# The second layer's projected inputs: inside attention, or at the head of the first feed-forward layer

## The chip, the cores and the metric

The kernel runs on one core of a Trainium2 chip. A core has five engines, each with its own queue of instructions that it works through in order: TensorE (PE, matrix products; its weight loads, PEld, overlap them), VectorE (DVE, element-wise work), ScalarE (ACT, activation functions and copies), GpSimd (POOL) and SyncE (SP, which issues nearly all transfers here). An instruction waits at the head of its queue for the results it needs and holds up all that stands behind it. Products are summed in PSUM, eight banks of 128 × 512 numbers; PE cannot write a bank again before another engine has read it.

The metric is the device time of one launch in microseconds (us). Before the change: 1715.05 us, the median of 3 runs (1713.93 to 1715.07).

## What is computed

A small encoder of two layers, 768 tokens in all (sequences of 512 and 256, kept side by side), model width 1024. Layer 0 mixes tokens by windowed attention, layer 1 by a gated convolution; each is followed by a feed-forward layer (1024 to 4096, squared rectifier, back to 1024) and by a gated input of its own:

```python
for i in range(DEPTH):
    h = rms_norm(x, norm_mix[i])
    x = x + (window_attention(h, ...) if i % 2 == 0 else short_conv(h, ...))
    h = rms_norm(x, norm_mlp[i])
    x = x + jnp.square(jax.nn.relu(h @ mlp_w_up[i])) @ mlp_w_down[i]
    gate = jax.nn.sigmoid(rms_norm(x, norm_ple[i]) @ ple_w_gate[i])
    x = x + (p[i] @ ple_w_proj[i]) * gate
return rms_norm(x, final_norm)
```

`p[i] @ ple_w_proj[i]`, the projected inputs, is a product of 768 × 256 by 256 × 1024. It depends on nothing else in the program, so it can be computed anywhere before the last step of its layer. The change concerns `p[1] @ ple_w_proj[1]`, which is needed near the end of the kernel.

## The kernel before

**Precision.** Every operand of a large product is split into a high part (a copy by ScalarE in a reduced format, L83 or L409) and a low part (the rest, a subtraction on VectorE, L84 or L420). A product is three matmuls: high by high, high by low, low by high.

**Layout.** Activations lie transposed: eight blocks of 128 channels × 768 tokens. In attention a product covers the tokens as 512 + 256 (`group`, L138), everywhere after it as two halves of 384 in two banks (`both`, `group2`, L129).

**Projected inputs.** `step` (L486) computes one block of 128 output channels: 12 weight loads, each streaming all tokens. The result is copied out of PSUM by ScalarE (or VectorE, for half of the first layer's) and stored to DRAM (`pj`), from where `gated` (L1109) fetches it much later. The first layer's eight steps are done at the very start while inputs load. The second layer's stand in attention: the inputs are split after the last block of head group 0 (`inputs1`), and the eight steps come after the last block of head group 1 (`projected(0)`, `projected(1)`).

**Attention** works through four groups of heads with six blocks of 128 queries each (`attend`, L639). In a block, PE makes scores (L667, L668); VectorE adds the bias and finds the maximum (L669); ScalarE exponentiates (L689); VectorE and ScalarE scale (L697, L695); PE transposes (L702); ScalarE and VectorE split (L710, L711); PE multiplies by the values (L712, L713); ScalarE and VectorE move the sum to `heads` (L715, L720). Other work is listed in `beside` to be issued after certain blocks: queries, keys, projections, the first part of the output. In this part a scheduler orders the instructions of every engine by its own estimates, the listed place being only a preference. At the end a loop of eight output products (24 or 12 weight-and-half pairs, 144 matmuls in all) finishes the residual stream block by block, in the order of `PAIRED`; `norm.block` then squares, scales and splits each block for the feed-forward layer, and `behind(i)` hangs further work after the i-th block.

**Feed-forward layer** (`mlp`, L853). The order of ACT, PE and DVE is written by hand here (`manual_schedule`). The hidden width is worked through in 16 chunks of 256; after each two come two `down` products. A chunk is either plain (`up_plain`, L897: 96 matmuls of 384 tokens) or a product by Strassen's scheme with seven part products instead of eight (`up`, L956: 84 matmuls). The second kind needs sums of blocks of the weights (`sums32`, `sums14`: VectorE) and of the activations (`norm.combine`, L301: two scaled copies and two high parts on ScalarE, four additions and two low parts on VectorE, for each of four pairs of blocks). `PLAIN` says how many of the first chunks of each layer are plain: three in layer 0, two in layer 1. `weave` interleaves several chains of steps. Work of chunk u's output that needs not be done at once is kept in `pend` and issued during the next.

In layer 0 chunk 0 runs before the statistics of the norm (`rstd_steps`: ones-matmuls at L226, a table load, logarithm, exponential, one Newton step) are known; its own output is scaled after them, and the four `combine` steps are spread over chunks 0 and 1.

**Buffers that matter.** Raw weights: three buffers (`wraw`). Split weights: two (`whi`, `wlo`), and one more of each under the tags `z` and `v`. PSUM after attention: four banks of tag A (two pairs), two of C, two of B; a new pair of a tag waits until the old one has been read. The six buffers of `big` hold passing results.

Of the kernel before, what the change touches and what calls it, by code (L numbers as in the profile page):

```python
# [11 lines left out]
F32 = mybir.dt.float32  # L12
# [6 lines left out]
P = 128  # L19
D = 1024  # L20
KB = D // P
# [26 lines left out]
def trunk_kernel(ctx: ExitStack, tc: tile.TileContext, a: dict, out: bass.AP):  # L48
# [397 lines left out]
    def mixer_attention():  # L446
# [10 lines left out]
        def pair(j, name, dt=F32):  # L457
            return main.tile([P, 2, T], dt, tag=f"x{j}", name=name)
# [24 lines left out]
                yield ps[:, :n], o, o + n  # L483
                o += n

        def step(i, w, part, tag, vector):  # L486

            l, m = i // KB, i % KB
            if tag == "L":
                t = ap.tile([P, T], F32, tag="L", name="pjs", bufs=BL)  # L490
            else:
                t = big("pjs")
            for ps, o, e in products(terms_of(w, part, col=m % 4 * P)):
                if vector:
                    dve.tensor_copy(t[:, o:e], ps)
                else:
                    act.activation(t[:, o:e], ps, AF.Copy)
            nc.sync.dma_start(pj[l][m], t[:])

        with tc.manual_schedule(engines=order):  # L500
            w0 = wp.tile([P, CH], F32, name="wraw", bufs=3)
            p0 = []
            for k in range(2):
                c = slice(512 * k, 512 * k + 512)
                nc.sync.dma_start(w0[:, c], a["proj"][0, 0, :, c])
                t = big("p")
                nc.sync.dma_start(t[:], a["p"][0, :, k, :])
                p0.append(t)
            w1 = fetch(a["proj"][0, 1])
            nc.sync.dma_start(vec[:], a["vec"][:])  # L510
# [12 lines left out]
            lo = wp.tile([P, CH], F32R, name="wlo", bufs=2)  # L523
            part0 = [], []
            for k in range(2):
                c = slice(512 * k, 512 * k + 512)
                split(hi[:, c], lo[:, c], w0[:, c])
                ph, pl = slot(10 + k, "p0h"), slot(12 + k, "p0l")
                split(ph[:], pl[:], p0[k][:])
                part0[0].append(ph[:])  # L530
                part0[1].append(pl[:])
            w0 = blocks(hi[:], 2), blocks(lo[:], 2)
            w1 = weight(None, 2, raw=w1)
            for i in range(KB):
                step(i, (w0, w1)[i // 4], part0, "L", i % 2)
                norm.block(i, xin(i))
                if i == 3:
                    wk = weight(None, KB, raw=wk)
                    wq = [fetch(a["w_q"][0])]

            bp = psum.tile([P, 512], F32, tag="S", name="bp", bufs=2)
            pe.matmul(bp[:HEADS, :], lhsT=rb[:], rhs=oh[:], start=True, stop=True)
            brow = tmp.tile([HEADS, 512], F32, tag="t", name="brow")
            dve.tensor_tensor(brow[:], bp[:HEADS, :], mk[:], ALU.add)
            kps = list(products(terms_of(wk, xs)))
            wq[0] = weight(None, KB, raw=wq[0])
            ss = norm.sum_squares(psum)

        with s1:
# [206 lines left out]
            def keys1():  # L756
                keys(1, products(terms_of(weight(a["w_k"][1], KB), xs)))

            def projected(q):
                w = weight(a["proj"][1, q], 2)  # L760
                for i in range(4):
                    step(KB + 4 * q + i, w, part1, "t", False)

            part1 = [], []

            def inputs1():
                ps = [pair(2 + p, "p1", F32R) for p in range(2)]
                for k in range(2):
                    t = fetch(a["p"][1, :, k, :])
                    split(ps[0][:, k, :], ps[1][:, k, :], t[:, :T])  # L770
                    for p in range(2):
                        part1[p].append(ps[p][:, k, :])

            def begin_output():
                for g in range(2):
                    split_heads(g)


            beside = {
                (0, 5): (inputs1, keys1),  # L780
                (1, 5): (lambda: projected(0), lambda: projected(1)),
                (2, 5): (begin_output, first_output),
            }
            for g in range(KV - 1):
# [37 lines left out]
        return Weights7(a["up"][l, f], a["up"][l, f + 2], plain=u < PLAIN[l])  # L822


    PLAIN = 3, 2

    def weave(*chains):

# [21 lines left out]

    ET = mybir.EngineType

    def mlp(l, norm, nxt, w, places, early):  # L853


        xs = norm.xs
# [40 lines left out]
        def up_plain(u, w, make, then):  # L897

            nonlocal r

            ps = [both(f"p{i + 1}", {0: "AA", 1: "BC"}.get(u, "AA")[i]) for i in range(2)]
            y1 = y2 = None

            def rects(*which):
# [2 lines left out]


            order = [(0, (0, 6), (0, 1)), (1, (0, 6), (0, 1)), (0, (6, 8), (0, 1)), (1, (6, 8), (0, 1))]
            if u > 0:  # L910
                order = [(i, (0, 8), (o,)) for o in (1, 0) for i in range(2)]
            for n, (i, ks, sides) in enumerate(order):
                for k in range(*ks):
                    m, h = PAIRED[k] % (KB // 2), PAIRED[k] // (KB // 2)
                    c = slice(P * m, P * m + P)
                    hi, lo = w.w[f"w{i + 1}{h + 1}"]
                    for j, (wt, part) in enumerate(((hi, 0), (hi, 1), (lo, 0))):
                        for o in sides:
                            pe.matmul(
                                ps[i][o],  # L920
                                lhsT=wt[:, c],
                                rhs=xs[f"x{h + 1}{1 + o}"][m][part],
                                start=k == 0 and j == 0,
                                stop=k == KB - 1 and j == 2,
                            )
                if n == 0:
                    v = make()
                    split2 = [lambda: v.split("second")] if v.plain else []
                    todo1 = norm.combine(todo.pop(0)) if todo else []
                    rest, pend[:] = pend[:4], pend[4:]  # L930
                    weave(rest, todo1, split2)
                elif n == 1:
                    if r is None:
                        parts = norm.acc_parts()
                    sums = [] if v.plain else [v.sums32, v.sums14, lambda: v.split("direct")]
                    weave(norm.combine(todo.pop(0)) if todo else [], sums, pend)
                    pend.clear()
                elif n == 2:
                    v.split("direct" if v.plain else "s32")
                    if u > 0:  # L940
                        y1, y2 = big("y1"), big("y2")
                        rects((0, 1), (1, 1))
                else:
                    if r is None:
                        steps = norm.rstd_steps(psum, norm.sum_squares(psum, parts=parts, tag="C"))
                        weave(steps, norm.combine(todo.pop(0)) if len(todo) > 1 else [])
                        r = norm.r
                        y1, y2 = big("y1"), big("y2")
                        rects((0, 1), (1, 1))
                    rects((0, 0))  # L950
                    squared(y1)
                    rects((1, 0))
                    pend.extend(acts_of(u, y1, y2, y2))
# [122 lines left out]
                        add(m, ps[i])  # L1076
                        nxt.block(m, x(m))

        jobs = [(up_plain, 0), (up_plain, 1)]
        for g in range(NG - 1):  # L1080
            jobs += [(up if 2 * g + 2 >= PLAIN[l] else up_plain, 2 * g + 2), (down, g, 0), (down, g, 1), (up, 2 * g + 3)]
        with tc.manual_schedule(engines={ET.Activation, ET.PE, ET.DVE}):
            for i, (job, *args) in enumerate(jobs):

                def make():
# [145 lines left out]

    xs0 = [*range(32, 42), *range(8, 15), *range(16, 20), *range(7)]
    act0 = [7, *range(20, 24), 28, 29, *range(24, 28), 15, 30, 31]

    held = xs0[17:] + act0 + [xs0[16]]
# [2 lines left out]


    n1 = Norm7(2, "mlp0", xs0, act0[7:11], act0[11])
    w0, behind = first_chunk(0, n1, 0)
    w = [weight(a["w_o0"][2], 4), weight(a["w_o2"], 2)]
    for i, m in enumerate(PAIRED):
        if i == 4:
# [7 lines left out]
        n1.block(m, x(m))  # L1254
        behind(i)
    n2 = Norm(4, "ple0", xs0[:16], xs0[16])
    mlp(0, n1, n2, w0[0], act0, 0)
    n3 = Norm(1, "mix1", xs0[17:] + act0[:5], act0[5])
    ple(n2, n3, act0[6:9])

# [91 lines left out]
```

## Time and profile before

| | us |
|---|---|
| median of 3 runs | 1715.05 |
| the profiled execution | 1715.87 |
| its span, first to last instruction | 1714.1 |
| TensorE busy | 1672.0 (98%) |
| VectorE busy | 1339.6 (78%) |
| ScalarE busy | 855.7 (50%) |
| granted TensorE clock, mean | 0.992 |

The mean clock hides three short spells of half clock after the start: from 158.3 us for 3.4 us, from 349.4 for 10.2, and at the very end. Times in the profile count from the first instruction. In the lists below a row of a timeline holds start, duration, engine, line, operation, what it writes and reads (names without buffer numbers), shapes and a count of merged instructions; in brackets the idle time before it and what ended that. Matmuls are pipelined, so the duration of one is longer than the step from one to the next. A row of busy times holds the stretch, its length, and then, for PE, PEld, DVE, ACT and POOL in this order, busy time and number of instructions; then the granted clock, the share of the DMA engines and GB/s.

Attention's first block begins its product by the values at 82.60 us. The output loop starts at 285.22, the feed-forward layer at 310.37, and its first `down` product at 373.72.

### The profile page before, as it was taken

The numbers are of one execution on the slowest core, as the hardware profiler recorded it, in microseconds if no ns is written. First come the engines' busy times: TensorE is split into PE (matmuls) and PEld (weight loads), VectorE is DVE, ScalarE is ACT, GpSimd is POOL, SyncE is SP. The second block draws the span as 40 slices with busy tenths as digits, with TensorE's granted clock in tenths as the row PEclk, the third lists the DMA queues.
The fourth block names the chain that finished last, engine by engine and source line by source line (L and its number), as shares of the span: only waits on it lengthen the run. The fifth ranks groups of instructions, "written<-read, shape, count | busy, mean of one in ns | idle before, by whom it ended". The sixth has DMA issues, their size and how long they took to land. (4 is left out here: it accounts for less than half of the span.)

```text
span 1714.1 us, 24208 instructions
## 1 busy us (share of the span) xinstructions
PE 1672.0 (98%) x9554; PEld 1616.8 (94%) x9554; DVE 1339.6 (78%) x2198; ACT 855.7 (50%) x1363; POOL 2.0 (0%) x30
## 2 busy tenths in 40 slices
PE   8999999979999999999999999999999999999996
PEld 7887878979999999999999999999999999999986
DVE  7587788878999999977764444667989999999676
ACT  6467756645455455545541111445455555545454
POOL 0000000000000000000000000000000000000000
PEclk9999999989999999999999999999999999999998
DMA  8653331112221222122312121211221222222222
GB/s 263 189 146 110 114 109 62 45 50 74 65 84 62 75 74 74 62 84 93 108 62 62 62 62 62 76 60 49 74 73 64 74 75 74 65 71 86 74 89 96
DMA packets 47554, 143.80 MB, mean 84 GB/s; under 512 B 6048, under 2 KB 10656, under 8 KB 47440
## 3 DMA queue, kind: packets, MB, share of 16 engines
q1 hardware_dynamic: 44880, 139.10, 25.8%
q10 hardware_dynamic: 2560, 3.15, 0.7%
q8 instruction: 75, 1.23, 0.3%
q14 instruction: 39, 0.32, 0.1%
HBM read 122.31 MB, written 10.48 MB: 77 GB/s over the span
## 5 line engine op out<-in xcount | busy, mean ns | idle before, releaser
L83 ACT ACTIVATE whi<-wraw 128x1024 fp32r<-128x1024 f32 (+2 forms) x74 | 76.6, 1035 | 183.9 <-PE b L129 53.2
L409 ACT ACTIVATE whi<-sum 128x1024 fp32r<-128x1024 f32 x55 | 57.9, 1053 | 146.6 <-PE a L441 146.6
L866 ACT ACTIVATE y<-y 128x768 f32<-128x768 f32 x64 | 53.4, 838 | 140.5 <-DVE y L863 140.5
L84 DVE TENSOR_TENSOR wlo<-wraw,whi 128x1024 fp32r<-128x1024 f32 (+2 forms) x74 | 88.2, 1191 | 11.7 <-ACT whi L83 11.4
L441 PE MATMUL a<-act,whi 128*128 128x384 f32 x448 | 96.7, 337 | 0.0
L441 PE MATMUL a<-t,zhi 128*128 128x384 f32 x440 | 90.7, 337 | 1.8 <-ACT c L967 1.8
L441 PE MATMUL b<-t,zhi 128*128 128x384 f32 x440 | 90.5, 337 | 0.9 <-DVE y L863 0.9
L441 PE MATMUL a<-t,whi 128*128 128x384 f32 x440 | 90.5, 337 | 0.0
L1023 DVE TENSOR_TENSOR x<-x,a 128x384 f32<-128x384 f32 x112 | 60.8, 553 | 35.1 <-PE a L441 34.8
L441 PE MATMUL a<-xs,whi 128*128 128x384 f32 x432 | 84.5, 337 | 0.0
L138 PE MATMUL mm<-xs_mix,whi 128*128 128x512 f32 (+1 forms) x320 | 83.3, 342 | 0.0
L441 PEld LDWEIGHTS a<-t,zhi 128*128 128x128 f32 x440 | 77.9, 188 | 2.1 <-ACT c L967 2.1
L441 PEld LDWEIGHTS a<-act,whi 128*128 128x128 f32 x448 | 79.8, 188 | 0.0
L441 PEld LDWEIGHTS b<-t,zhi 128*128 128x128 f32 x440 | 77.7, 188 | 1.2 <-issue 1.2
L441 PEld LDWEIGHTS a<-t,whi 128*128 128x128 f32 x440 | 77.8, 188 | 0.0
L441 PEld LDWEIGHTS a<-xs,whi 128*128 128x128 f32 x432 | 76.3, 188 | 0.0
L420 DVE TENSOR_TENSOR wlo<-wraw,whi 128x1024 fp32r<-128x1024 f32 x60 | 73.0, 1217 | 1.9 <-ACT whi L409 1.9
L420 DVE TENSOR_TENSOR wlo<-sum,whi 128x1024 fp32r<-128x1024 f32 x55 | 67.2, 1222 | 9.2 <-ACT whi L409 9.2
L409 ACT ACTIVATE whi<-wraw 128x1024 fp32r<-128x1024 f32 x60 | 63.2, 1054 | 17.4 <-issue 10.3
L420 DVE TENSOR_TENSOR zlo<-sum,zhi 128x1024 fp32r<-128x1024 f32 x55 | 66.9, 1217 | 1.9 <-ACT zhi L409 1.9
L409 ACT ACTIVATE zhi<-sum 128x1024 fp32r<-128x1024 f32 x55 | 58.3, 1060 | 19.9 <-DVE sum L385 16.1
L330 ACT ACTIVATE t<-y 128x768 fp32r<-128x768 f32 x56 | 47.0, 841 | 40.6 <-DVE y L321 27.9
(279 smaller groups left out, 4647.9 us busy)
## 6 DMA issues: line engine op xcount, KB each, us to landing
wraw<-in_up SPq DMA_DIRECT2D x64, 512.0 KB, 3.5
wraw<-in_down SPq DMA_DIRECT2D x64, 512.0 KB, 3.5
wraw<-in_w_in SPq DMA_DIRECT2D x24, 512.0 KB, 3.4
wraw<-in_gate SPq DMA_DIRECT2D x16, 512.0 KB, 3.5
pj<-pjs SPq DMA_DIRECT2D x16, 384.0 KB, 2.9
wraw<-in_w_q SPq DMA_DIRECT2D x8, 512.0 KB, 4.9
wraw<-in_w_out SPq DMA_DIRECT2D x8, 512.0 KB, 3.4
x_in<-in_x SPq DMA_DIRECT2D x8, 384.0 KB, 7.2
```

Source lines behind the costliest of these rows:

```text
L83: first = act.activation(hi, src, AF.Copy)
L84: dve.tensor_tensor(lo, src, hi.bitcast(F32), ALU.subtract)
L138: pe.matmul(ps[:, o:e], lhsT=w, rhs=x[:, o:e], start=i == 0 and j == 0, stop=i == n - 1 and j == 2,)
L330: act.activation(t[0][:], (self.q1, self.q2)[i][:], AF.Copy)
L409: act.activation(hi[:], src, AF.Copy)
L420: dve.tensor_tensor(lo[:], src, hi[:].bitcast(F32), ALU.subtract)
L441: pe.matmul(ps, lhsT=a, rhs=b, start=start and i == 0, stop=i == len(terms) - 1, skip_group_check=True)
L866: act.activation(t[:], t[:], AF.Square)
L1023: dve.tensor_tensor(t[:, o : o + H], t[:, o : o + H], f, op)
```

## The change

The eight steps of the second layer's projected inputs leave attention and are issued between attention's output loop and the first chunk of layer 0's feed-forward part. Their inputs are loaded and split after the first two blocks of the output loop, the first half of their weights after its fifth, the second half at the first step. Each step uses a pair of banks (`"AABCAABA"` gives the tags) and two copies of 384 tokens by ScalarE. Between the steps stand three of the four `combine` steps, the accumulator's split, the split of chunk 0's weights (which stood in the output loop) and the ones-matmuls; the statistics are finished right after. So chunk 0 begins with the statistics known, in the order that until now only later chunks had; the fourth `combine` is done during it. `PLAIN` for layer 0 goes from 3 to 1: chunks 1 and 2 use the seven products. The list of slots for layer 0 is reordered so that four slots, free until the fourth `combine`, hold the split inputs.

```diff
-        def step(i, w, part, tag, vector):
+        def step(m, w, part, vector):
...
             beside = {
-                (0, 5): (inputs1, keys1),
-                (1, 5): (lambda: projected(0), lambda: projected(1)),
+                (0, 5): (keys1,),
                 (2, 5): (begin_output, first_output),
             }
...
-    PLAIN = 3, 2
+    PLAIN = 1, 2
...
+    def second_inputs(places):
+        part = [], []
+        ws = []
+        def behind(i):
+            if i < 2:
+                raw = fetch(a["p"][1, :, i, :])
+                hi, lo = (slot(places[2 * i + p], "p1") for p in range(2))
+                split(hi[:], lo[:], raw[:, :T])
+                part[0].append(hi[:])
+                part[1].append(lo[:])
+            if i == 4:
+                raw = fetch(a["proj"][1, 0])
+                hi, lo = (more.tile([P, CH], F32R, tag=f"z{p}", name=f"z{p}", bufs=1) for p in ("hi", "lo"))
+                split(hi[:], lo[:], raw[:])
+                ws.append((blocks(hi[:], 2), blocks(lo[:], 2)))
+        def product(m):
+            if m == 0:
+                ws.append(weight(a["proj"][1, 1], 2))
+            ps = both("pj", "AABCAABA"[m])
+            group2(ps, terms_of(ws[m // 4], part, col=m % 4 * P))
+            return ps
+        return behind, product
+
+    def ahead(norm, product, places):
+        w = None
+        ps = []
+        def copied(m):
+            t = slot(places[m % 4], "pjs", F32)
+            for f, o, e in pieces(ps[m]):
+                act.activation(t[:, o:e], f, AF.Copy)
+            nc.sync.dma_start(pj[1][m], t[:])
+        for m in range(KB):
+            ps.append(product(m))
+            if m == 0:
+                w = up_chunk(0, 0)
+            else:
+                copied(m - 1)
+            if m in (0, 2, 5):
+                weave(norm.combine((0, 2, 5).index(m)))
+            elif m == 3:
+                parts = norm.acc_parts()
+            elif m == 4:
+                w.split("direct")
+            elif m == 6:
+                w.split("second")
+                ss = norm.sum_squares(psum, parts=parts, tag="C")
+        copied(KB - 1)
+        return w, ss
...
+            known = r is not None
...
-            if u > 0:
+            if known:
                 order = [(i, (0, 8), (o,)) for o in (1, 0) for i in range(2)]
...
-        jobs = [(up_plain, 0), (up_plain, 1)]
+        ups = [(up if u >= PLAIN[l] else up_plain, u) for u in range(2 * NG)]
+        jobs = ups[:2]
...
         with tc.manual_schedule(engines={ET.Activation, ET.PE, ET.DVE}):
+            if product:
+                w, ss = ahead(norm, product, places[5:7] + places[12:])
+                todo = todo[-1:]
+                r = norm.rstd(psum, ss)
...
-    xs0 = [*range(32, 42), *range(8, 15), *range(16, 20), *range(7)]
+    xs0 = [*range(32, 42), *range(8, 15), *range(7), *range(16, 20)]
...
-    w0, behind = first_chunk(0, n1, 0)
+    behind, product = second_inputs(xs0[24:])
...
-    mlp(0, n1, n2, w0[0], act0, 0)
+    mlp(0, n1, n2, None, act0, 0, product)
```

More of the change, by code (lines that the diff above doesn't have):

```diff
@@ L484, in products @@
                 o += n
-        def step(i, w, part, tag, vector):
[L488 to L492, printed above, removed]
+        def step(m, w, part, vector):
+            t = ap.tile([P, T], F32, tag="L", name="pjs", bufs=BL)
             for ps, o, e in products(terms_of(w, part, col=m % 4 * P)):
@@ L497, in step @@
                     act.activation(t[:, o:e], ps, AF.Copy)
-            nc.sync.dma_start(pj[l][m], t[:])
+            nc.sync.dma_start(pj[0][m], t[:])
         with tc.manual_schedule(engines=order):
@@ L534, in mixer_attention @@
             for i in range(KB):
-                step(i, (w0, w1)[i // 4], part0, "L", i % 2)
+                step(i, (w0, w1)[i // 4], part0, i % 2)
                 norm.block(i, xin(i))
@@ L757, in keys1 @@
                 keys(1, products(terms_of(weight(a["w_k"][1], KB), xs)))
[L759 to L772, printed above, removed]
             def begin_output():
@@ L851, in trunk_kernel, with mlp @@
     ET = mybir.EngineType
-    def mlp(l, norm, nxt, w, places, early):
+    def second_inputs(places):
[45 more added lines that the diff above has]
+        return w, ss
+    def mlp(l, norm, nxt, w, places, early, product=None):
         xs = norm.xs
@@ L932, in up_plain @@
                 elif n == 1:
-                    if r is None:
+                    if not known:
                         parts = norm.acc_parts()
@@ L939, in up_plain @@
                     v.split("direct" if v.plain else "s32")
-                    if u > 0:
+                    if known:
                         y1, y2 = big("y1"), big("y2")
@@ L943, in up_plain @@
                 else:
-                    if r is None:
+                    if not known:
                         steps = norm.rstd_steps(psum, norm.sum_squares(psum, parts=parts, tag="C"))
@@ L1077, in last_down @@
                         nxt.block(m, x(m))
-        jobs = [(up_plain, 0), (up_plain, 1)]
+        ups = [(up if u >= PLAIN[l] else up_plain, u) for u in range(2 * NG)]
+        jobs = ups[:2]
         for g in range(NG - 1):
-            jobs += [(up if 2 * g + 2 >= PLAIN[l] else up_plain, 2 * g + 2), (down, g, 0), (down, g, 1), (up, 2 * g + 3)]
+            jobs += [ups[2 * g + 2], (down, g, 0), (down, g, 1), ups[2 * g + 3]]
         with tc.manual_schedule(engines={ET.Activation, ET.PE, ET.DVE}):
+            if product:
+                w, ss = ahead(norm, product, places[5:7] + places[12:])
+                todo = todo[-1:]
+                r = norm.rstd(psum, ss)
             for i, (job, *args) in enumerate(jobs):
```

## The prediction

> **What bounds the kernel now.** I read the page first, then the busy time by stretch, then the timelines of the places that the change touches.
>
> ```profile
> PE 1672.0 (98%) x9554; PEld 1616.8 (94%) x9554; DVE 1339.6 (78%) x2198; ACT 855.7 (50%) x1363; POOL 2.0 (0%) x30
> ...
> wraw<-in_up SPq DMA_DIRECT2D x64, 512.0 KB, 3.5
> ...
> pj<-pjs SPq DMA_DIRECT2D x16, 384.0 KB, 2.9
> ```
>
> TensorE (PE) is busy for 98% of 1714.1 us, so a change pays by taking matmuls out or by closing one of PE's few idle places. The stretches show them; the columns are length, then busy time of PE, weight loads, VectorE (DVE), ScalarE (ACT) and GpSimd, then the granted clock.
>
> ```profile
> 154.04:168.42 14.38, 10.86 (x52) 8.43 (x52) 9.80 (x27) 10.16 (x27) 0.00 (x0) 0.88 0.73 220
> 168.42:187.50 19.08, 19.01 (x106) 15.81 (x104) 10.15 (x37) 12.39 (x30) 0.00 (x0) 1.00 0.50 179
> 187.50:216.33 28.83, 27.99 (x175) 24.38 (x174) 25.26 (x75) 22.84 (x59) 0.00 (x0) 1.00 0.26 72
> ...
> 285.22:310.37 25.15, 25.15 (x144) 25.15 (x145) 21.38 (x33) 15.86 (x22) 0.00 (x0) 1.00 0.20 64
> 310.37:344.60 34.23, 34.23 (x197) 34.09 (x196) 26.54 (x40) 22.55 (x29) 0.00 (x0) 1.00 0.15 47
> 344.60:360.00 15.40, 6.02 (x20) 5.33 (x19) 13.35 (x20) 7.71 (x11) 0.00 (x0) 0.67 0.20 68
> ```
>
> From 154 to 187.5 us the second layer's projections run inside attention: PE is busy there, VectorE for 20 of 33.5 us. From 285 PE has no gap (attention's output loop, then the first two plain chunks) until 344.6, where it stands still:
>
> ```profile
> 310.37 0.34 PE L919 MATMUL p<-xs,zhi 128*128 128x384 f32 x1
> ...
> 344.44 0.34 PE L919 MATMUL p<-xs,wlo 128*128 128x384 f32 x1
> 352.79 1.01 PE L919 MATMUL p<-x,zhi 128*128 128x384 f32 x2 [8.01 <-ACT zhi L409]
> 355.17 0.69 PE L919 MATMUL p<-x,zlo 128*128 128x384 f32 x1 [1.37 <-DVE zlo L420]
> ...
> 373.72 0.87 PE L441 MATMUL a<-act,whi 128*128 128x384 f32 x4
> ```
>
> The third plain chunk waits 8.01 us for the high half of its weights and 1.37 for the low one. That split stands in ScalarE's queue behind the norm's statistics, the outputs of chunks 0 and 1 and the norm's sums (`combine`). At 373.72 the first down product begins; from there both kernels issue the same work.
>
> **The change, part by part.**
>
> *Fewer matmuls.* From 310.37 to 344.44 lie 195 steps (192 matmuls of two plain chunks, 4 of the norm): 0.175 us each. A plain chunk has 96 (16.8 us), one by seven products 84 (14.7 us). Chunks 1 and 2 change from the first to the second: **−4.2 us** of work, and the hole at 344.6 has no third plain chunk left to stand before.
>
> *The projections leave attention:* 8 steps of 12 weight loads over 768 tokens, 2.1 us each at that pace, so 16.8 us of PE; with them 16 copies on ScalarE, four splits on both engines, 4 loads and 8 stores. How much of it attention gives back is set by the other engines. In 154.04 to 216.33 PE is busy 57.9 us (10.86+19.01+27.99) and VectorE 45.2. Without the projections PE needs 41 and VectorE, less two weight splits of 1.2, about 43. They become equal, and VectorE is the bound. In the changed program's order this is plain: the queries of the third head group are issued earlier, and its first four blocks follow each other with no other matmul between. Their VectorE work, from the rows for all 24 blocks (56 key blocks):
>
> ```profile
> L711 DVE TENSOR_TENSOR pl<-pt,ph 128x512 fp32r<-128x512 f32 x56 | 36.4, 685 | 8.6 <-ACT ph L710 8.4
> L669 DVE CUSTOM_DVE_ANT_0 L<-S,bias,sink 128x256 f32<-128x256 f32 x61 | 27.6, 476 | 2.1 <-DMA bias<-skew 1.1 <-PE S L668 0.8
> L720 DVE TENSOR_TENSOR heads<-O,ot 64x256 f32<-64x256 f32 x48 | 19.9, 415 | 9.3 <-ACT ot L715 8.8
> L669 DVE CUSTOM_DVE_ANT_0 L<-S,bias,sink 128x384 f32<-128x384 f32 x32 | 18.6, 611 | 4.1 <-PE S L668 3.1 <-ACT L L689 0.8
> L697 DVE TENSOR_SCALAR L<-L,sm 128x256 f32<-128x256 f32 x48 | 14.2, 348 | 0.2
> L697 DVE TENSOR_SCALAR L<-L,sm 128x384 f32<-128x384 f32 x24 | 8.9, 414 | 0.1
> ```
>
> Busy time over count, a block of two key blocks takes 4×0.45 + 2×0.65 + 2×0.41 + 3×0.30 = 4.8 us, one of three 6.2, so the four 22 us, where PE has half as much to do. The bounds of the gain: above, all of PE's time, 16.8 us; below, 6.0 us, if these four blocks keep VectorE no busier than 154.04:168.42 does (the last rival prices it). I take VectorE's best share in this mix, 25.26/28.83 = 0.88: 43/0.88 = 48.9 us instead of 62.3, a gain of **13.4 us**.
>
> *The output loop* gets the two splits of the inputs and one of the projection weights in place of a chunk's two. Its PE time is 25.15 us without a gap. Two more loads go through the three raw buffers, so ScalarE waits for the projection weights before the first norm block, and the loop's second weights come later:
>
> ```profile
> 296.74 1.23 DVE L84 TENSOR_TENSOR wlo<-wraw,whi 128x1024 fp32r<-128x1024 f32 x1
> ```
>
> I work this low half out to end some 5 us later than now, at 302.6 in this execution's time; in the new order its first matmul is the 99th of the loop, 17 us after 285.22, so at 302.4. 0 to 2 us, **+0.5**.
>
> *The projections at the head* bring their 16.8 us, now as two halves of 384, with 0.7 of the norm's matmuls. PE's own work to the first down product is then 17.5 + 16.8 + 2×14.7 = 63.7 us, as much as the 63.35 that the whole stretch takes now with its hole. So every wait that is left counts. ScalarE's and VectorE's rows in the order of the queue:
>
> ```profile
> 310.22 1.06 ACT L409 ACTIVATE whi<-wraw 128x1024 fp32r<-128x1024 f32 x1 [0.72 <-PE mm L129]
> 311.19 0.60 ACT L290 ACTIVATE xs<-x,vec 128x384 fp32r<-128x384 f32 x1
> 312.20 0.83 ACT L195 ACTIVATE sq<-x 128x768 f32<-128x768 f32 x1
> 312.94 0.92 ACT L295 ACTIVATE xs<-x,vec 128x768 fp32r<-128x768 f32 x1
> ...
> 320.00 0.84 ACT L83 ACTIVATE ah<-acc_mlp 128x768 fp32r<-128x768 f32 x1
> 320.74 0.92 ACT L303 ACTIVATE q<-x,vec 128x768 f32<-128x768 f32 x1
> 324.37 0.85 ACT L330 ACTIVATE t<-q 128x768 fp32r<-128x768 f32 x1 [0.40 <-DVE q L326]
> 329.82 1.28 ACT L242 ACT_TABLE_LOAD   x1
> 375.76 0.84 ACT L1018 ACTIVATE C<-a 128x384 f32<-128x384 f32 x2
> ...
> 314.87 0.95 DVE L196 TENSOR_TENSOR acc_mlp<-acc_mlp,sq 128x768 f32<-128x768 f32 x1
> 315.74 2.35 DVE L420 TENSOR_TENSOR wlo<-wraw,whi 128x1024 fp32r<-128x1024 f32 x2
> 323.12 0.56 DVE L325 SCALAR_TENSOR_TENSOR q<-q 128x384 f32<-128x384 f32 x1
> 324.19 2.01 DVE L336 TENSOR_TENSOR t<-q,t 128x768 fp32r<-128x768 f32 x2
> 334.95 0.96 DVE L259 SCALAR_TENSOR_TENSOR rstd_mlp<-v,y 128x768 f32<-128x768 f32 x1
> ```
>
> Instructions of one engine that don't depend on each other follow some 0.08 us sooner than they last (two low halves of 1.22 take 2.35). Time 0 is the first projection product. Projections 0 to 3 fill their four pairs of banks by 8.4; each later one needs a copy by ScalarE to free a pair.
> - Copy 0 is queued behind the second projection weights' split (it waits for PE's last matmul of the loop, as at 310.22), the last two blocks of the norm, and the first `combine`: two q of 0.83, then two highs that wait for VectorE. VectorE ends the norm's last block at 5.4 now (314.87 + 0.95 − 310.37); with the two q in ScalarE's queue ahead of that block it is 7. Then a low half (1.15) and four steps of 0.58; the second high starts at 10.4, copy 0 is done at 12.1. PE waits 3.8 us.
> - Copy 2 stands behind the second `combine` (again q, q, four VectorE steps, two highs): done at 17.9 when PE is at 16.3, 1.6 us.
> - Copy 4, behind the accumulator's split, copy 3 and a weight split: 21.3 against 20.8, 0.5 us.
> - The plain chunk needs the pair of copy 5, behind the third `combine`: 26.4 against 23.4, 3.0 us.
> - The chunk ends at 43.2. The next one's first bank is free when VectorE has read it. ScalarE reaches the table load at 28.9, after copy 7, and from there the statistics take 6.1 us (329.82 to 334.95 + 0.96). At 35 VectorE goes on with the last `combine`, four weight sums and two low halves, and has read the bank at 45.6: 2.4 us.
>
> Sum of waits 11.3, so the first down product stands at 75.0 instead of 63.35: **+11.6 us**. Bounds: 0 if ScalarE kept up, +14 if each of some 25 hand-overs between the engines costs 0.1 us more than I gave it. I take the worked value, since it has the pace of the same instructions at the same place. SyncE's queue adds nothing: the eight stores (2.9 us each) have four buffers, and the load for the next chunk that stands among them can go at 22 and lands 3.5 later, long before its sums at 39.
>
> *Sum:* −13.4 + 0.5 + 11.6 = −1.3 (the −4.2 is in the 63.7). The profiled execution took 1715.87 (span 1714.1 and 1.8 around it), 0.8 over the median of 1715.05. So 1714.6 for such an execution, and **1713.7** beside the median.
>
> The Trainium skill's page "TensorE: Matmul & The Clock Gate" (section "Part 1: The HAM clock gate") says that PE's clock is halved after an idle window of about 3.4 us and restored after a busy one. The trace agrees with the halving: 0.67 after the hole of 8 us. By that rule the 3.8 us wait would cost about 1.7 us (an estimate from the page's window), unless it falls into the next wait; the second rival below prices this from rows.
>
> **The rivals.** One run tells no change from 0.2%, 3.4 us, on either side.
> - *Attention gives back all of PE's time,* 16.8 us: −16.8 + 0.5 + 11.6 = −4.7, 1710.3. For it: PE at 98%, and the waits between projection and copy (a stretch at clock 0.88) go too. Against: the 22 us of VectorE.
> - *The clock drops in the head or in the four blocks.* The stretch from 344.6 has (1 − 0.67)/0.5 × 15.4 = 10.2 us of half clock; if 3.8 of such a spell lie in a wait, the rest costs 3.2 us: 1716.9.
> - *The head doesn't stall:* ScalarE stays within half of each wait that I worked out, −5.7: 1708. For it: its busy share is 22.55/34.23 in the same place now. Against: its queue is in order, and each copy stands behind a chain through VectorE.
> - *Slower: the four blocks without other matmuls run at the pace of their chain* (scores, maximum, exponent, scaling, transposition, product, each on another engine), at VectorE's 9.80/14.38 = 0.68 instead of 0.88: 22/0.68 − 22/0.88 = +7.4 us, 1721. It decides as soon as VectorE idles in a block for more than a fifth. For it: that is what 154.04:168.42 did. Against: there PE also stood waiting for the projections' copies.
>
> **How the numbers follow.** The worked sum 0.36, all of PE's time 0.20, head without stall 0.12, clock 0.08, blocks at their chain's pace 0.24. The sum's own errors (2 us in the head, 2 in attention) put a little of it beyond −3.4: faster 0.36 (0.20 + 0.12 + 0.04), same 0.38 (the rest of the sum, and most of the clock case), slower 0.26. Cases of both signs hold over half of it; the likeliest one's own range is 1710 to 1717. The range reaches from the head without stall to the slow blocks: 1707 to 1721.5.
>
> **What would show it.** In the profile after: output loop starting about 13 us earlier, VectorE busy 0.85 or more and PE about half busy in the third group's first four blocks; no wait before L919's old third chunk; in the head, PE waiting for ScalarE's copies of the projections four times, 9 us in all, and once for VectorE before the first seven-product chunk; the first down product 75 us after the loop's end. A loop that starts less than 8 us earlier, or a head below 68 us, proves me wrong.

## The result, and the profile after

The changed kernel takes **1720.05 us** (median of 11 runs, 1717.61 to 1720.73); the kernel before, run beside it, 1715.76 (11 runs, 1713.93 to 1718.55). The ratio is 1.0023, 95% interval 1.0014 to 1.0033: slower by 2.4 to 5.7 us, where 1713.7 was forecast beside 1715.05.

The profiled executions took 1720.73 us (span 1718.7) and 1715.87 (1714.1). Their 4.6 us of span divide up like this:

| stage | before | after | difference | forecast |
|---|---|---|---|---|
| start to the output loop | 285.22 | 276.90 | −8.3 | −13.4 |
| output loop | 25.15 | 25.96 | +0.8 | +0.5 |
| loop's end to the first down product | 63.35 | 74.63 | +11.3 | +11.6 |
| from there to the end | 1340.38 | 1341.21 | +0.8 | 0 |

So the other three terms came within 0.8 us of the forecast, and attention gave back 5.1 us too little. The engines' busy time and the busy time by stretch of the changed kernel (columns as before: length; PE, PEld, DVE, ACT, POOL; clock, DMA share, GB/s):

```profile
PE 1676.3 (98%) x9530; PEld 1614.8 (94%) x9530; DVE 1349.9 (79%) x2212; ACT 860.6 (50%) x1373; POOL 2.0 (0%) x30
```

```profile
154.46:183.81 29.35, 27.97 (x155) 22.32 (x154) 23.48 (x71) 20.14 (x52) 0.00 (x0) 1.00 0.44 121
183.81:206.57 22.76, 17.33 (x88) 11.84 (x87) 21.76 (x73) 18.66 (x52) 0.00 (x0) 1.00 0.37 109
206.57:276.90 70.33, 67.93 (x379) 56.82 (x379) 57.41 (x159) 41.78 (x102) 0.00 (x0) 0.95 0.19 54
276.90:302.86 25.96, 25.86 (x144) 25.03 (x145) 20.23 (x31) 13.53 (x19) 0.00 (x0) 1.00 0.31 102
302.86:328.36 25.50, 19.61 (x101) 17.27 (x100) 20.86 (x30) 19.27 (x31) 0.00 (x0) 1.00 0.33 120
328.36:346.94 18.58, 18.58 (x97) 18.30 (x97) 14.00 (x20) 12.20 (x17) 0.00 (x0) 0.91 0.29 97
346.94:377.49 30.55, 29.72 (x169) 29.26 (x169) 27.41 (x41) 18.28 (x26) 0.00 (x0) 1.00 0.20 66
```

The second row is the third group's first four blocks: VectorE is busy for 21.76 of 22.76 us, as forecast the bound, and PE has 88 matmuls where the stretch 154.46:183.81 has 155. The third row, the rest of attention, lasts 70.33 us; in the kernel before the same blocks (216.33 to 285.22) took 68.89 with more work for VectorE:

```profile
216.33:285.22 68.89, 66.65 (x387) 56.16 (x387) 59.25 (x167) 42.37 (x107) 0.00 (x0) 1.00 0.27 81
```

What differs for the worse is the clock (0.95 against 1.00); run 7 prices it. In smaller stretches the changed kernel's trace gives:

```profile
200.21:203.63 3.42, 3.11 (x12) 1.67 (x11) 3.21 (x13) 2.89 (x11) 0.00 (x0) 1.00 0.55 159
203.63:207.04 3.41, 1.59 (x10) 1.04 (x9) 3.38 (x10) 2.71 (x9) 0.00 (x0) 1.00 0.33 121
207.04:213.87 6.83, 6.19 (x16) 4.30 (x16) 5.09 (x11) 1.94 (x6) 0.00 (x0) 0.50 0.57 149
213.87:216.14 2.27, 2.27 (x20) 2.16 (x18) 1.65 (x5) 1.09 (x2) 0.00 (x0) 1.00 0.25 79
```

At the end of the four blocks PE works for 1.59 of 3.41 us; then it is given half its clock for 6.83 us, just when the output's first products come up (from one matmul of 512 tokens to the next it takes 0.43 us there and 0.23 after it).

From the output loop to the first down product PE's waits, summed by what ended them (engine, tile and line that waited, releaser; total, times, longest), and where those of the head stand in PE's timeline (the one for `xa` is ahead of the loop's first product):

```profile
PE pj L129 <- ACT pjs L870: 3.2, 2, 1.7
PE p L958 <- ACT pjs L870: 2.6, 1, 2.6
PE mm L129 <- DVE xa L732: 1.2, 1, 1.2
PE a L441 <- ACT c L1006: 0.8, 1, 0.8
```

```profile
313.86 1.18 PE L129 MATMUL pj<-p,whi 128*128 128x384 f32 x4 [1.70 <-ACT pjs L870]
...
320.04 1.18 PE L129 MATMUL pj<-p,whi 128*128 128x384 f32 x4 [1.47 <-ACT pjs L870]
...
328.36 0.62 PE L958 MATMUL p<-x,zhi 128*128 128x384 f32 x2 [2.55 <-ACT pjs L870]
...
346.94 1.63 PE L441 MATMUL a<-xs,whi 128*128 128x384 f32 x8
```

The copies (L870) hold PE up three times, 5.7 us in all. The plain chunk then lasts 18.58 us instead of 16.8, at clock 0.91.

### The profile page after: what moved, and what is told of

It reads as the page before. It is cut to its first block, busy times and chain, and to the rows that moved or that the text cites. A ratio compares the mean times of both kernels' runs of the same rounds, so it can differ in the third digit from the quotient of the medians.

```text
span 1718.7 us, 24188 instructions
## 1 busy us (share of the span) xinstructions
PE 1676.3 (98%) x9530; PEld 1614.8 (94%) x9530; DVE 1349.9 (79%) x2212; ACT 860.6 (50%) x1373; POOL 2.0 (0%) x30
## 5 line engine op out<-in xcount | busy, mean ns | idle before, releaser
L441 PE MATMUL a<-t,zhi 128*128 128x384 f32 x456 | 94.5, 339 | 2.7 <-ACT c L1006 2.7
L84 DVE TENSOR_TENSOR wlo<-wraw,whi 128x1024 fp32r<-128x1024 f32 (+2 forms) x73 | 86.9, 1190 | 7.9 <-ACT whi L83 7.7
L441 PE MATMUL a<-xs,whi 128*128 128x384 f32 x464 | 90.7, 337 | 0.0
L441 PEld LDWEIGHTS a<-xs,whi 128*128 128x128 f32 x464 | 81.7, 188 | 0.3 <-issue 0.3
L409 ACT ACTIVATE whi<-wraw 128x1024 fp32r<-128x1024 f32 x60 | 63.2, 1054 | 16.9 <-issue 10.3
```

The source lines that it names most:

```text
L84: dve.tensor_tensor(lo, src, hi.bitcast(F32), ALU.subtract)
L409: act.activation(hi[:], src, AF.Copy)
L441: pe.matmul(ps, lhsT=a, rhs=b, start=start and i == 0, stop=i == len(terms) - 1, skip_group_check=True)
```

## The experiments

The theories after this reading: attention is held up by VectorE and by PE's clock once its filling is gone; the head is held up by the copies in ScalarE's queue. Rivals: it is merely the order of the work; it is the chain of engines in a block; in the head it is the norm's sums on VectorE. All runs in one table. Medians stand beside the kernel before, whose own median was 1716.0 to 1716.6 in these series; the stages are from each profile ("attention": first block's product by the values to the loop; "half clock": spells in it).

| kernel | median, us | ratio to before, 95% | attention | half clock | loop | head |
|---|---|---|---|---|---|---|
| before | 1715.76 | | 202.62 | 3.4 | 25.15 | 63.35 |
| after | 1720.05 | 1.0014–1.0033 | 194.97 | 6.8 | 25.96 | 74.63 |
| attn_alone | 1705.88 | 0.9925–0.9950 | 194.36 | 6.8 | 25.15 | 63.22 |
| head_no_copies | 1713.11 | 0.9969–0.9987 | 194.50 | 6.8 | 25.99 | 68.79 |
| combine_early | 1715.32 | 0.9988–1.0006 | 193.52 | 3.4 | 25.91 | 70.34 |
| fill_spread | 1716.68 | 0.9994–1.0012 | 192.44 | 3.4 | 26.73 | 73.59 |
| plain_two | 1717.50 | 0.9996–1.0014 | 204.31 | 6.8 | 25.16 | 62.87 |
| clock_kept | 1717.17 | 0.9993–1.0010 | 192.42 | none | 26.68 | 74.33 |
| spread_and_two | 1713.56 | 0.9976–0.9994 | 195.43 | 10.2 | 29.04 | 67.56 |
| half_and_half | 1720.20 | 1.0015–1.0034 | 197.03 | 3.4 | 29.03 | 67.66 |
| scale_moved | 1712.41 | 0.9965–0.9985 | 190.06 | 3.4 | 25.16 | 73.62 |
| kept_and_early | 1713.28 | 0.9972–0.9990 | 192.44 | none | 26.31 | 70.68 |
| kept_early_scale | 1713.29 | 0.9974–0.9992 | 194.37 | 3.4 | 25.69 | 70.30 |
| before_scale | 1717.19 | 0.9996–1.0014 | 203.24 | 3.4 | 25.17 | 62.66 |
| scale_early | 1707.95 | 0.9940–0.9965 | 189.66 | 3.4 | 25.18 | 70.26 |

**1. Attention's part alone.**

```diff
-                (0, 5): (inputs1, keys1),
-                (1, 5): (lambda: projected(0), lambda: projected(1)),
+                (0, 5): (keys1,),
...
```

> The kernel before without the second layer's projections: attention, in the order of the changed kernel, leaves them out, nothing takes their place, and the head keeps its three plain chunks (the last step of layer 1 uses the first layer's projections). Theory: attention gives back only 8.3 us of the 16.8, because the queries' products are drawn forward and the third group's first four blocks then run at VectorE's pace; so the output loop starts at 277 us (before: 285.2), lasts 25.15, the first down product stands 63.4 later, and the time is 8.3 below the kernel before. Rival 1, the prediction on record: 13.4 us, loop at 272. Rival 2: what attention gives back is lost again later, because the transfers or the clock of the head stand differently: head 67 us or more, time less than 5 us below before.

Measured: 10.3 us below before by the medians (8.6 to 12.9, so a little more than the 8.3 expected), loop at 276.05, head as before. The theory's stages hold; PE's order in attention is that of the changed kernel. Neither 13.4 nor 16.8 came back, nor was any of it lost again in the head. The profiles differ by 9.6 us, 0.9 of them ahead of the first block.

**2. Strassen's part alone.**

```diff
-    PLAIN = 3, 2
+    PLAIN = 2, 2
```

> The kernel before with two plain chunks instead of three in the first feed-forward layer, nothing moved: one part of the change alone. Theory: PE's work falls by the 2.1 us that a chunk by seven products saves, but the third chunk now needs all four combine steps and the sums of its weights ahead, which stand in the same queues; PE's hole before it stays at 8 us or grows, from the loop's end to the first down product 61 to 65 us (before: 63.35), time within 2 us of the kernel before. Rival: the shorter chunk pays in full and the hole doesn't grow: 61.2 us, time 2.1 below before.

PE's waits in the third chunk of this kernel, from its timeline:

```profile
354.71 2.93 PE L441 MATMUL a<-xs,whi 128*128 128x384 f32 x8 [7.07 <-ACT whi L409]
...
361.32 2.56 PE L441 MATMUL b<-t,zhi 128*128 128x384 f32 x8 [2.28 <-DVE y L863]
```

The hole of 9.4 us is still there, now 7.07 and 2.28, and the time didn't fall: the queues decide there, not PE's work. Its attention, the same program as before's, took 1.7 us more with one more spell of half clock.

**3. The head without the copies.**

```diff
-            for f, o, e in pieces(ps[m]):
-                act.activation(t[:, o:e], f, AF.Copy)
-            nc.sync.dma_start(pj[1][m], t[:])
...
```

> The changed kernel without the copies of the projections out of PSUM and without their stores; the products themselves stay at the head (the last step of layer 1 uses the first layer's projections). Theory: the head's waits hang on these copies in ScalarE's queue; without them PE needs its 63.7 us of work and at most 3 more from the loop's end to the first down product (74.6 with them), there is no spell of half clock in the first chunk, and the time is 8 to 11 us below the changed kernel's 1720. Rival: the waits hang on the norm's sums (combine) and VectorE, busy for 82% there, would only move them to the first chunk by seven products: 71 us or more, less than 4 us gained.

The head fell by 5.8 us, half of what it had grown by, and the time by 6.9: between the two expectations. PE and VectorE at the first chunk by seven products:

```profile
340.01 1.65 PE L441 MATMUL a<-xs,whi 128*128 128x384 f32 x8 [1.85 <-DVE y L898]
```

```profile
338.17 1.22 DVE L420 TENSOR_TENSOR zlo<-sum,zhi 128x1024 fp32r<-128x1024 f32 x1
339.31 1.95 DVE L898 SCALAR_TENSOR_TENSOR y<-p,rstd_mlp 128x384 f32<-128x384 f32 x4
```

PE now reaches that chunk 1.85 us before VectorE has read its bank. So VectorE's queue (last combine, sums and low halves of the weights, then this reading) is a second bound close behind the copies. In the changed kernel the same reading stands at L901, and PE's chunk begins at 346.94, as soon as the first of its four parts is done:

```profile
346.24 1.94 DVE L901 SCALAR_TENSOR_TENSOR y<-p,rstd_mlp 128x384 f32<-128x384 f32 x4
```

There the plain chunk at half clock filled the wait, and that spell cost nothing.

**4. The head with one combine step less.**

```diff
...
+            if i == 5:
+                weave(norm.combine(0))
...
-            if m in (0, 2, 5):
+            if m in (2, 5):
...
```

> The changed kernel with the first of the norm's four combine steps hung behind the sixth block of the output loop and taken out of the head. Theory: ScalarE's queue in the head is shorter by 3.4 us and VectorE's by 4.3 ahead of copy 0, so PE's first wait for a copy (2.0 us at the fifth projection) goes and the next ones halve: head 74.6 to 70 or 71; the loop, in which VectorE is busy for 20.2 of 26.0 us and ScalarE for 13.5, becomes 0 to 1.5 us longer; time 1716 to 1718. Rival: VectorE has no room in the loop, which becomes longer by as much as the head wins: 1720.

As expected in the stages: head 4.3 us shorter, loop not longer (25.91). The time is 4.7 us below the changed kernel, a little more than expected; attention, with one spell of half clock less, is 1.5 us shorter.

**5. Half of the projections in each place.** Projections 0 to 3 as before in attention, 4 to 7 at the head, one combine step in the loop, and two of them, not one, behind the norm's statistics.

> The changed kernel with the first four projections back in attention, where the kernel before had them, and the last four at the head; one combine step hung behind the loop's sixth block. Theory: 8.4 us of PE's work and four copies fit beside attention's blocks, where PE stands idle for 25 us: attention from its first block to the loop 195 to 198 us (195.0 with none of the projections, 202.6 with all); head with 55.3 us of PE's work and 3 to 6 of waits; time 1709 to 1712. Rival: what is put back in attention lengthens it by its own 8.4 us, since the four blocks without other matmuls are VectorE's: 202 or more, time 1714 to 1718.

Attention did as the theory has it (197.03); the head didn't, and the time is that of the changed kernel, above both expectations:

```profile
344.91 1.30 PE L441 MATMUL a<-xs,whi 128*128 128x384 f32 x3 [6.79 <-DVE y L917]
```

With 8.4 us less work in the head PE waits 6.79 us for VectorE at the same place, and 2.96 ahead of the first projection for VectorE's addition in the loop (busy for 24.75 of 29.03 us). The half that left the head isn't the only difference: with a combine step more, VectorE takes 13.0 us from the end of the statistics to the reading that frees this bank, against 9.0 in the changed kernel. And the head has two spells of half clock of 6.8 us, from 308.1 and 342.2; the last 4.1 us of the second lie behind that wait. What both this miss and run 3 show is that PE's work isn't the bound in the head, so that work taken away there gains less than it weighs.

**6. Other work beside the four blocks.** The queries of group 4 and the output's first products listed after blocks 0, 1, 2, 3 and 5 of the third group.

```diff
...
+            for n, f in zip((0, 0, 1, 1, 2, 3, 5), [lambda: queries(6), lambda: queries(7), begin_output, *parts]):
+                beside[2, n] = (*beside.get((2, n), ()), f)
...
```

> The changed kernel with the work beside attention's blocks listed otherwise: the queries of the fourth group after the third group's first block, and the first part of the output in four pieces after its blocks 1, 2, 3 and 5, instead of all of it after block 5; the same instructions, in another order. Theory: attention's shortfall is one of order: PE alone is the bound up to 176 us, then VectorE alone for four blocks (busy for 21.8 of 22.8 us). With matmuls beside these blocks PE loses 14 to 19 us to waits between the first block and the loop instead of 26.8, the spell of half clock at 207 us goes, the loop starts at 265 to 270 instead of 276.9, and the time is 1708 to 1713. Rival: VectorE's total or the chain through the engines in each block is the bound, whatever stands beside: loop at 275 or later, 1718 or more.

Between the two: loop at 273.58 us, attention 192.44. The four blocks grew to 35 us, and what was saved later is little more:

```profile
182.55:217.61 35.06, 33.57 (x188) 27.42 (x189) 29.33 (x91) 20.75 (x59) 0.00 (x0) 0.95 0.28 88
217.61:273.58 55.97, 50.42 (x284) 40.18 (x283) 49.20 (x146) 39.35 (x100) 0.00 (x0) 1.00 0.18 51
```

The matmuls that fill these blocks are missing behind them (PE 50.42 of 55.97 us, VectorE 49.20). So this other order brings 2.5 us of attention, with a spell of half clock less in it, and not the 5.1 that were missing.

**7. PE kept at work in its idle time.** 80 transposes that nobody reads:

```diff
...
+                for i in range(20):
+                    pe.transpose(t[:, i % 4 * P : i % 4 * P + P], heads[2][:, i % 2, b * P : b * P + P], ident[:])
...
+            beside[2, 4] += tuple(lambda b=b: dummy(b) for b in range(4))
```

> The changed kernel with 80 idle transposes on PE (4 blocks of 20, 0.109 us each, of the third group's own finished heads, into a bank that nobody reads) listed so that they fall into PE's idle time beside the third group's first four blocks; the order of all else stays. Theory: the spell of half clock from 207 to 214 us comes from PE's idleness before it and costs most of the 3.4 us of PE's work that it takes: with the transposes there is no such spell, the four blocks stay at 22.8 us within 0.7, from the fifth block's product by the values to the loop 70.3 becomes 67.5 to 69, and the time falls by 1.5 to 3 from the changed kernel's 1720. Rival: VectorE and the chain through the engines are the bound there, and PE's slower clock lies in its idle time: 70.3 within 0.5, or later where the transposes stand in the way.

```profile
182.12:206.16 24.04, 23.02 (x166) 20.00 (x166) 22.89 (x74) 18.15 (x49) 0.00 (x0) 1.00 0.40 111
206.16:272.73 66.57, 65.26 (x384) 55.64 (x382) 55.95 (x158) 42.23 (x105) 0.00 (x0) 1.00 0.18 54
```

More work on PE, and 2.9 us less time. The four blocks take 1.3 us longer, the rest of attention 66.57 instead of 70.33, at full clock. The order did not stay as it was: behind the blocks the scheduler put the output's products otherwise, some of them earlier. A second reading is free of that: in the attention of after, attn_alone, head_no_copies and combine_early PE has the same matmuls in the same order; with 6.8 us at half clock it took 194.97, 194.36 and 194.50, with 3.4 193.52, and the part behind the four blocks 70.33, 69.84 and 69.99 against 69.05. By that 3.4 us at half clock cost 1.1 us, by before and plain_two (one order too) 1.7, by fill_spread and spread_and_two (3.4 and 10.2 us of half clock) 1.5. Twice that is an estimate for the spell of 6.8: 2.2 to 3.4 us. So of the 3.8 us by which the rest of attention became shorter with the transposes, 0.4 to 1.6 are left for the order.

**8. VectorE relieved.** With the change, and without it:

```diff
-NA = 1
+NA = 2
```

> The changed kernel with NA = 2: of each block's four scalings by the sum of the exponents ScalarE does two and VectorE two, instead of one and three. That takes 0.35 to 0.41 us a block from VectorE (21.8 of 22.8 us busy in the third group's first four blocks, 0.83 over the last 122 us of attention) and gives ScalarE 0.5 to 0.6 (18.7 of 22.8). Theory: VectorE bounds attention where matmuls beside it are missing; the four blocks fall from 22.8 to 20.8 to 21.8 us, attention from its first block to the loop from 195.0 to 189 to 193, time 1715 to 1718. Rival: not VectorE's load but the chain through the engines, in which ScalarE's longer scaling stands, sets the pace: four blocks 22.8 or more, attention 194.5 or more, time 1719 or more.

> The kernel before with NA = 2 (ScalarE does two of each block's four scalings instead of one), nothing else changed. Theory: with the projections beside its blocks attention is PE's (busy for 0.95 of the last 131 us, VectorE 0.80), and VectorE becomes the bound only once they are gone; so what took 4.9 us from the changed kernel's attention takes at most 2 here: attention from its first block to the loop 200.5 to 203.5, time 1713.5 to 1717. Rival: the gain came from another order of the instructions, or from VectorE's load whatever stands beside it: attention 199 or less, time 1710 to 1713.

After the change it takes 4.9 us from attention (of them, by run 7, 1.1 to 1.7 for one spell less), in the kernel before nothing (203.24). The busy time of the whole end of attention, changed kernel first, then scale_moved, then the kernel before, then before_scale:

```profile
154.46:276.90 122.44, 113.23 (x621) 90.97 (x620) 102.65 (x301) 80.58 (x204) 0.00 (x0) 0.97 0.29 80
```

```profile
154.74:271.46 116.72, 110.24 (x609) 87.61 (x609) 98.03 (x284) 84.91 (x215) 0.00 (x0) 0.99 0.29 83
```

```profile
154.04:285.22 131.18, 124.51 (x716) 104.77 (x715) 104.47 (x301) 87.77 (x220) 0.00 (x0) 0.99 0.35 109
```

```profile
152.32:285.91 133.59, 125.83 (x723) 106.33 (x723) 100.65 (x289) 94.99 (x236) 0.00 (x0) 0.99 0.35 107
```

Where the projections are gone, 4.6 us less of VectorE come with a stretch 5.7 us shorter; where they stand, PE is busy for 125.83 of 133.59 us, and 3.8 us less of VectorE gain nothing. That a longer scaling on ScalarE went with a shorter attention speaks against the chain of a block as the bound. The scheduler's order changed in both kernels, so the order isn't ruled out as a cause of a part of the 4.9 us. Two expectations missed: the time fell below 1715, and the four blocks didn't get shorter (26.16 us); 22 of the output's matmuls now stand in them.

**9. Put together.** Each edit is one shown above; spread_and_two has a second combine step in the loop.

> The changed kernel with the idle transposes of clock_kept and the early combine step of combine_early. Theory: the shortfall in attention (clock) and the waits in the head (queues) are apart, so their gains of 2.9 and 4.7 us add up: attention 192.4 us from its first block to the loop, 96.3 from there to the first down product, time 1711.5 to 1713.5, below the kernel before. Rival: the clock that is kept in attention, or the work that is now denser in the loop, is paid in the head: time 1715 or more.

> The changed kernel with the work beside attention's blocks listed as in fill_spread, and two of the four combine steps hung into the output loop, behind its fourth and seventh blocks. Theory: the two causes are apart and add up: attention 192.4 us from the first block to the loop, loop 27 to 30 us (VectorE has 5 us of room there and gets 9), loop's end to the first down product 64 to 67; time 1709 to 1713. Rival: VectorE, 21.4 of 26.6 us busy in the loop, hands on what it gets: loop and head together 96 us or more, time 1714 or more.

> kept_and_early with NA = 2 as in scale_moved. Theory: with PE's clock kept VectorE is what is left to bound attention, so the 8 us of work taken off it are worth 2 to 5 us: attention 187.5 to 190.5, time 1707 to 1711. Rival: ScalarE's longer chain takes it back: attention 192 or more, time as kept_and_early or above.

> The changed kernel with NA = 2 as in scale_moved and one combine step in the loop as in combine_early. Theory: the two limits, VectorE in attention and the copies' queue in the head, are apart: attention 190 us, loop and head 94.5 to 96, time 1707 to 1709.5, below both kernels. Rival: the loop's VectorE has no room when it starts earlier, or the order in attention changes as it did in kept_early_scale: 1711 or more.

kept_and_early came about as the sum of its parts. In spread_and_two, between its two expectations, the second combine step in the loop does no better than the first alone: what the head wins (67.56), the loop loses (29.04); and attention, in fill_spread's order, took 195.43 instead of 192.44 with 10.2 us of half clock instead of 3.4. The transposes and NA = 2 don't add up: the numbers are those of the rival, but its cause isn't shown; the trace has another order and a spell of half clock at 181.6 us, and what decides there wasn't tried further. One combine step in the loop with NA = 2, no transposes, is the best that computes everything: **1707.95 us** (median of 5 runs), 6.0 to 10.3 below the kernel before and 12.1 below the changed one.

```profile
81.02:270.68 189.66, 183.21 (x1055) 151.37 (x1054) 158.68 (x470) 139.77 (x356) 0.00 (x0) 0.99 0.33 92
270.68:295.86 25.18, 25.18 (x144) 25.18 (x145) 22.38 (x35) 16.57 (x23) 0.00 (x0) 1.00 0.31 105
295.86:335.55 39.69, 36.77 (x198) 35.63 (x197) 32.39 (x45) 29.46 (x45) 0.00 (x0) 0.96 0.35 122
335.55:366.12 30.57, 29.74 (x170) 29.32 (x170) 27.44 (x41) 18.27 (x26) 0.00 (x0) 1.00 0.20 66
```

Attention is 5.3 us shorter than in the changed kernel, the head (the last two rows) 4.4.

## Why the prediction was wrong

- **The step that failed** is the attention term: "I take VectorE's best share in this mix, 25.26/28.83 = 0.88: 43/0.88 = 48.9 us instead of 62.3, a gain of **13.4 us**." It gave 8.3. VectorE did bound the four blocks (0.96), and its share over the whole came out as taken: from 154.46 to 206.57 it was busy for 23.48 + 21.76 = 45.24 of 52.11 us, 0.87. That agreement is partly luck, since up to 183.81 PE was the bound (27.97 of 29.35 us, VectorE 0.80). Two things were missing. VectorE had 2.2 us more to do there than my 43, for four of the output's splits of 0.95 us were drawn forward into the stretch, against one weight split of 1.22 us less (the rest of attention has 57.41 of VectorE instead of 59.25). And this would have come back later, but there PE had half its clock for 6.8 us: the rest took 70.33 instead of 68.89 us. So 10.2 us were gained up to 206.57, 1.4 given back behind, and 0.4 lost ahead of 154.
- **The clock** was in the text as a rival (0.08, +3.2, "in the head or in the four blocks"), not in the sum. The price was about right: an estimated 2.2 to 3.4 us in attention (run 7). The chance wasn't: I forecast PE half busy in those blocks and didn't ask what its clock makes of that. In the head the spell came too and cost nothing, in place of the 2.4 us that I had PE wait for VectorE.
- **The slow blocks** (0.24) didn't come: VectorE at 0.96 there, not 0.68. The time fell near that rival's 1721 by another mechanism.
- **All of PE's time back** and **the head without stall** fell; run 1 and the head's 74.63 us say so.
- **Loop and head** held, +0.8 and +11.3 for +0.5 and +11.6, the head by luck: its parts were off and balanced. Beside PE's 63.7 us, the copies cost three waits of 1.7, 1.5 and 2.6 us instead of four of 8.9 in all; the clock took 1.8 in the plain chunk, where VectorE's wait was to take 2.4; 0.8 is a wait for ScalarE behind it; and some 2.6 stand in no listed wait and stay open. PE's work was sized rightly: a step of the projections is 12 matmuls, each over half of the tokens here, and takes 2.1 us. That the copies and VectorE's queue are two bounds close together (run 3) I had not seen; the sum holds for this queue order only.
- **Behind the first down product** I had nothing. The profile has 0.8 us there, about what the spell of half clock at 1190 us costs (below).

## What to carry to other kernels

Taking matmuls out of a stretch returns time only up to the next engine's bound, and a PE that then idles by halves may be given a slower clock just when its work comes back: price that in the sum, from the trace's own spells. Work that moves in front of an in-order queue costs by the queue, not by its own length. After such a move, balance the engines anew: the same relief of VectorE that gained nothing before came with 5 us after it, of which a part may be order and clock.

## What the runs showed of the hardware

Half clock didn't need an idle PE. Ahead of the spell at 207 us PE was busy for 1.59 of 3.41 us; in the 3.42 us before that for 3.11, and the clock stayed full. The Trainium skill's page "TensorE: Matmul & The Clock Gate" (section "Part 1: The HAM clock gate") speaks of an idle window of 3.4 us, and in that the measurement differs: a window with PE busy for a little under half of it was enough. With its other statement, that the windows run freely and the clock so varies from run to run, the traces agree: behind the first down product PE has the same matmuls in the same order in all 15 traces; six have a spell of 3.4 us that begins between 1178 and 1191 us and take 1340.8 to 1341.3 us for it, nine have none and take 1339.8 to 1340.5. From the changed kernel's trace:

```profile
1187.00:1194.00 7.00, 5.16 (x21) 4.83 (x20) 5.65 (x9) 5.05 (x10) 0.00 (x0) 0.76 0.06 8
```

Transposes held the clock up: in run 7, where 80 of them stand in the four blocks, PE was busy for 23.02 of 24.04 us and no spell came.
